# A fused attention layer on one core: the modulation and the first superblock's input by halves of the features, with the first halves of three chunks multiplied in between

## The chip, the cores and the metric

The kernel runs on one core of one Trainium2 chip. The metric is the device time of one execution in microseconds (us). Engines are named as the profile names them: PE is TensorE's matmul, PEld its weight load, DVE is VectorE, ACT is ScalarE, POOL is GpSimd, SP the engine that issues most DMAs.

## The reference

One decoder layer on x of 4096 rows and 1024 features:

```
shift, scale, gate = split(silu(c) @ w_ada + b_ada)
h    = rmsnorm(x, norm_g) * (1 + scale) + shift
proj = h @ w_in                      # 1024 x 3328, 26 chunks of 128 columns
y_sb = stick_breaking_attention(...) * silu(sb_g)     # 8 heads of 64
y_sw = sliding_window_sink_attention(...) * silu(sw_g) # 8 heads, 2 kv heads
x    = x + gate * (concat(y_sb, y_sw) @ w_out)
out  = rmsnorm(x, final_g)
```

The modulation needs c @ w_ada before the first h can be formed, and h before the first product with w_in.

## The kernel before

The rows are worked on in 8 superblocks of 512. Each matrix is split into two 16-bit parts, hi and lo, and a product is three passes: hi x hi, hi x lo, lo x hi. A chunk is 128 columns of w_in times the 512 rows: 8 feature tiles (k) x 3 passes = 24 matmuls of 128x128 by 128x512 into one PSUM bank (`mm`, four of them), written in items of two k. hT holds the superblock's input, transposed and split; w holds a chunk's weights, split by ACT (hi) and DVE (lo) in `stage_split`.

`setup_x0` makes the first superblock's hT. For the scale, then for the shift, DVE adds up eight rows blocks of w_ada, each times its element of silu(c), into `acc0` (`mod_part`, lines 125 and 127); `mod_cols` sums over the partitions on PE with a vector of ones (line 139, bank `pv`). With the scale, PE transposes the normalised rows and ACT writes xT (lines 171, 172); with the shift, ACT writes the hi part of hT (line 183) and DVE the lo part (line 184). a16 and s16, the scale and shift in columns, are also stored to DRAM (`arow`, `srow`, line 187), for the later superblocks.

For the first superblock the weights come from w_in in float32 (`stage_load`, line 273) through a ring `f` of four places, in the order `sorder`: SWK, SWG, SWG+1, SWG+2, SBV, SWQ, SBV+1, SWQ+1, SBV+2, SWG+3, SBV+3, SWV and so on. The four rows blocks of x take the same four places at first. The split weights lie in a ring `w` of three places, or for the v columns (SBV and its three followers, SWV) in `wv`; those of the ring are also stored to DRAM (`wsc`, line 293), for the later superblocks. `advance_w` loads one chunk and splits the oldest one loaded.

After `setup_x0`, `main` makes a list of work items: the chunks SWK, SWG, SWG+1, SWG+2, SWQ, then blocks of v (`v_items`, 24 matmuls each with all of SBV to SBV+3), further chunks, attention steps and output. On every second or fourth item a step of `setup_wo_items` is put in: eight loads of the gate's part of w_ada (`mod_load`, line 130), eight accumulates of the gate (lines 231 and 233) each followed by a load of w_out, a few small ones, and eight products of w_out with the gate (`wo`: two `wot` on DVE, line 254, then ACT and POOL). Near its end the first superblock's list also prepares the second superblock's input on PE (`x_items_pe`: `norm`, line 330, and transposes, line 400). Attention steps are placed among the items by times summed up from the items' estimates. Each engine runs its instructions in the order in which they are written; SP's DMAs share one queue.

Of the kernel before, what the change touches and what calls it, by code (L numbers as in the profile page):

```python
# [7 lines left out]
F32 = mybir.dt.float32  # L8
# [44 lines left out]
class Kern:  # L53
# [64 lines left out]

    def mod_part(self, which, k, st):

        nc = self.nc
        acc = self.acc0
# [11 lines left out]

    def mod_cols(self, which):
        nc = self.nc
        ps = self.P["pv"].tile([128, 512], F32, tag="pv", name="modps")
        for j in range(KD):
            nc.tensor.matmul(out=ps[:, j:j + 1], lhsT=self.acc0[:, j * 128:(j + 1) * 128], rhs=self.ones[:, 0:1],
                             start=True, stop=True)  # L140
        mod = self.const.tile([128, KD], F32, name=f"mod{which}")
        o = 16 + which * KD
        nc.vector.tensor_tensor(out=mod, in0=ps[:, 0:KD], in1=self.col[:, o:o + KD], op=ALU.add)
        return mod

    def setup_x0(self):

        nc = self.nc
        stage = self.wo.rearrange("p m e n -> p m (e n)").bitcast(F32)
        xs = [self.x_load(self.x[b * 128:(b + 1) * 128, :]) for b in range(2)]  # L150
        for k in range(KD):
            self.mod_load(1, k, stage[:, k])
        xs += [self.x_load(self.x[b * 128:(b + 1) * 128, :]) for b in range(2, NB)]
        xT = self.P["hT"].tile([128, KD, T], F32, tag="hT", name="xT")
        hT = self.new_hT(0)
        for b in range(2):
            self.x_norm(xs[b], hT[:, b, 0])
        self.run_later(9)
        for k in range(KD):
            self.mod_part(1, k, stage[:, k])  # L160
            self.mod_load(0, k, stage[:, k])
        for b in range(2, NB):
            self.x_norm(xs[b], hT[:, b, 0])
        self.run_later(9)
        scale = self.mod_cols(1)
        nc.vector.tensor_scalar(out=self.a16, in0=scale, scalar1=1.0, scalar2=HS, op0=ALU.add, op1=ALU.mult)
        nc.vector.tensor_tensor(out=self.a16, in0=self.a16, in1=self.col[:, 8:16], op=ALU.mult)
        for k in range(KD):
            ps = self.mm()
            for b in range(NB):  # L170
                nc.tensor.transpose(ps[:, b * 128:(b + 1) * 128], xs[b][:, k * 128:(k + 1) * 128], self.ident)
            nc.scalar.activation(xT[:, k, :], ps, AF.Identity, scale=self.a16[:, k:k + 1])
        self.stage_load()
        self.stage_load()
        self.stage_load()
        for k in range(KD):
            self.mod_part(0, k, stage[:, k])
        shift = self.mod_cols(0)
        self.stage_split()
        nc.vector.tensor_scalar(out=self.s16, in0=shift, scalar1=HS, scalar2=None, op0=ALU.mult)  # L180
        for k in range(KD):
            xk = xT[:, k, :].rearrange("p (b t) -> p b t", t=128)
            nc.scalar.activation(hT[:, :, 0, k, :], xk, AF.Identity, bias=self.s16[:, k:k + 1])
            nc.vector.scalar_tensor_tensor(out=hT[:, :, 1, k, :], in0=xk, scalar=self.s16[:, k:k + 1],
                                           in1=hT[:, :, 0, k, :], op0=ALU.add, op1=ALU.subtract)
        for row, col in ((self.arow, self.a16), (self.srow, self.s16)):
            nc.sync.dma_start(out=row.rearrange("o (k p) -> p (o k)", p=128), in_=col)
# [227 lines left out]

    def chunk_items(self, s, c, evac):
        nc = self.nc
# [298 lines left out]
    def main(self):  # L716
# [8 lines left out]
        self.sorder = [SWK, SWG, SWG + 1, SWG + 2, SBV, SWQ, SBV + 1, SWQ + 1, SBV + 2, SWG + 3, SBV + 3, SWV] + order[7:]  # L725
        self.spos, self.staged = [0, 0], []
        self.wpos = 0
# [8 lines left out]
        self.v[-1] = v0  # L736
        self.setup_x0()
        self.stage_load()
        self.stage_split()

# [19 lines left out]
        for s in range(NS):  # L760
# [15 lines left out]
            add([(0.0, lambda s=s: self.new_hT(s + 1))])  # L776
            step(self.chunk_items(s, SWK, self.evac_k(s, 4, "ksw")))
            for p in range(3):
                step(self.chunk_items(s, SWG + p, self.evac_g(s, 4 + p)))
            vi = self.v_items(s, s * NB)  # L780
# [279 lines left out]
```

## Time and profile before

| | |
|---|---|
| median of 3 runs | 1770.54 us (1769.33 to 1771.67) |
| the profiled execution | 1770.9 us, span 1769.2 us |
| PE busy | 1666.3 us (94%) |
| DVE, ACT, POOL busy | 1020.9, 725.0, 592.5 us |
| mean granted clock of PE | 0.98 |

Busy time is the time in which an engine works on an instruction; the span is that of the profiled execution on the chip, and about 1.7 us of its time lie around the span. A busy share over the whole span is a mean over stages with different limits.

### The profile page before, as it was taken

How to read it: one execution, taken by the hardware profiler on the slowest of the kernel's cores; microseconds unless marked ns; L12 is line 12 of the kernel's file. 1: busy time of each engine (PE TensorE's matmuls, PEld its weight loads, DVE VectorE, ACT ScalarE, POOL GpSimd, SP SyncE). 2: the span in 40 equal slices, each digit the busy share in tenths (PEclk: the TensorE clock that was granted, in tenths of full speed). 3: DMA queues.
4: the chain of work that ended last, by engine and by line, in shares of the span. 5: the costliest groups of instructions: out<-in, count | busy, mean ns of one | idle time of the engine just before them, and what ended most of it. 6: DMA issues, size and time to landing. Idle time of an engine off the chain costs nothing.

```text
span 1769.2 us, 28179 instructions
## 1 busy us (share of the span) xinstructions
PE 1666.3 (94%) x10790; PEld 859.7 (49%) x10790; DVE 1020.9 (58%) x1869; ACT 725.0 (41%) x1428; POOL 592.5 (33%) x745
## 2 busy tenths in 40 slices
PE   3798689999999999999999999999999999999987
PEld 2354345554554554554554445544545545545443
DVE  6467885565645566455645656455664557355562
ACT  3445653444335444343334443354433444244331
POOL 2023664432234323432234322442234323122231
PEclk9899879999999999999999999999999999999999
DMA  7877656466756757566665767567575756355552
GB/s 274 277 214 178 181 145 175 116 167 154 189 134 143 168 147 200 111 150 154 164 175 129 161 161 184 126 144 175 145 202 112 155 153 164 92 126 132 157 135 74
DMA packets 417126, 280.41 MB, mean 159 GB/s; under 512 B 341676, under 2 KB 368340, under 8 KB 416980
## 3 DMA queue, kind: packets, MB, share of 16 engines
q1 hardware_dynamic: 374692, 182.01, 44.0%
q10 hardware_dynamic: 42288, 96.49, 18.5%
q8 instruction: 87, 1.43, 0.3%
q14 instruction: 59, 0.48, 0.1%
HBM read 151.54 MB, written 27.80 MB: 101 GB/s over the span
## 4 chain that ended last, share of the span: by engine, by line
PE 74%; DVE 9%; ACT 6%; DMA 4%; POOL 3%; issue 3%; SPq 1%; ACTq 0%; POOLq 0%; DVEq 0%
PE mm L430 40%; PE mm L687 14%; PE mm L503 7%; PE pv L640 5%; PE z L555 4%; PE mm L515 2%; ACT p L599 2%; DMA q<-q 2%; DVE w L290 1%; DVE acc L127 1%; DMA f<-in_x_dram 1%; POOL p L608 1%; ACT hT L325 1%; DMA f<-in_w_in_dram 1%; DVE w L622 1%
## 5 line engine op out<-in xcount | busy, mean ns | idle before, releaser
L430 PE MATMUL mm<-hT,w 128*128 128x512 f16 x4032 | 914.2, 382 | 7.6 <-ACT w L289 2.8
L430 PEld LDWEIGHTS <-w 128*128 128x128 f16 x4032 | 389.0, 99 | 461.3 <-issue 17.6
L687 PE MATMUL mm<-wo,yT 128*128 128x512 f16 x1536 | 346.8, 381 | 0.0
L608 POOL TENSOR_SCALAR p<-p,smm 128x256 f32<-128x256 f32 x256 | 123.2, 502 | 432.8 <-DVE smm L606 302.9
L687 PEld LDWEIGHTS <-yT 128*128 128x128 f16 x1536 | 148.7, 98 | 171.7 <-issue 2.6
L658 POOL TENSOR_TENSOR yT<-gs,yT 128x256 f16<-128x256 f32 x128 | 142.7, 1115 | 248.4 <-DVE yT L657 233.6
L599 ACT ACTIVATE p<-sp,nm 128x256 f32<-128x256 f32 (+1 forms) x256 | 126.0, 493 | 222.2 <-DVE nm L592 222.0
L569 DVE TENSOR_TENSOR_SCAN nb<-nb,d 128x768 f32<-128x768 f32 x64 | 115.3, 1801 | 136.0 <-ACT nb L563 136.0
L565 POOL TENSOR_SCALAR_AFFINE_SELECT beta<-beta 128x512 f32<-128x512 f32 x64 | 90.2, 1410 | 283.4 <-ACT beta L564 243.1
L503 PE MATMUL mm<-wv,hT 128*128 128x512 f16 x768 | 174.9, 383 | 6.9 <-ACT wv L289 6.3
L503 PEld LDWEIGHTS <-hT 128*128 128x128 f16 x768 | 74.8, 98 | 93.6 <-issue 10.5
L622 DVE SCALAR_TENSOR_TENSOR w<-p,w 128x1024 f16<-128x1024 f32 x64 | 85.1, 1330 | 58.7 <-ACT w L621 58.7
L563 ACT ACTIVATE nb<-z 128x768 f32<-128x768 f32 x64 | 51.8, 810 | 160.4 <-PE z L555 93.0
L621 ACT ACTIVATE w<-beta 128x768 f16<-128x768 f32 x64 | 53.9, 842 | 153.8 <-DMA wT<-w 71.3
L640 PEld LDWEIGHTS <-v 128*64 128x64 f16 x2304 | 89.1, 110 | 55.3 <-issue 51.4
L592 DVE CUSTOM_DVE_ANT_0 sp<-z,bias,nsink 128x256 f32<-128x256 f32 (+1 forms) x256 | 107.2, 474 | 14.6 <-PE z L555 14.3
L640 PE MATMUL pv<-wT,v 128*64 128x128 f16 (+1 forms) x2304 | 110.1, 240 | 3.5 <-DVE yT L657 2.6
L621 ACT ACTIVATE w<-p 128x1024 f16<-128x1024 f32 x64 | 67.6, 1056 | 76.8 <-POOL p L608 39.7
L693 DVE SCALAR_TENSOR_TENSOR f<-mm,f 128x512 f32<-128x512 f32 x64 | 43.0, 675 | 86.9 <-DMA f<-in_x_dram 70.5
L494 DVE SCALAR_TENSOR_TENSOR v<-mm,v 128x512 f16<-128x512 f32 (+1 forms) x64 | 31.2, 488 | 97.3 <-ACT v L493 95.8
L555 PEld LDWEIGHTS <-q 128*128 128x128 f16 x768 | 68.4, 100 | 20.0 <-issue 3.2
L446 DVE SCALAR_TENSOR_TENSOR q<-mm,q 64x512 f16<-64x512 f32 x64 | 43.8, 684 | 59.2 <-ACT q L445 58.6
(113 smaller groups left out, 1737.1 us busy)
## 6 DMA issues: line engine op xcount, KB each, us to landing
w<-wsc ACTq DMA_DIRECT2D x147, 512.0 KB, 3.8
f<-in_x_dram SPq DMA_DIRECT2D x64, 512.0 KB, 4.6
q<-q ACTq DMA_DIRECT2D x128, 128.0 KB, 3.7
out_dram<-f SPq DMA_DIRECT2D x32, 512.0 KB, 3.6
f<-in_w_in_dram SPq DMA_DIRECT2D x26, 512.0 KB, 5.9
wo<-in_w_ada_dram SPq DMA_DIRECT2D x24, 512.0 KB, 8.0
wsc<-w SPq DMA_DIRECT2D x21, 512.0 KB, 5.3
wo<-in_w_out_dram SPq DMA_DIRECT2D x8, 512.0 KB, 5.7
```

Source lines behind the costliest of these rows:

```text
L430: nc.tensor.matmul(out=ps, lhsT=w[:, k, a, :], rhs=hT[:, :, b, k, :], start=(k == 0 and i == 0), stop=(k == KD - 1 and i == 2))
L503: nc.tensor.matmul(out=ps, lhsT=hT[:, tb, b, k, :], rhs=self.wv[:, k, a, 0:512], start=(k == 0 and i == 0), stop=(k == KD - 1 and i == 2))
L555: nc.tensor.matmul(out=o[:, k0:256], lhsT=q[:, j, h, cols], rhs=kt[:, kh, (qb - 1) * 128 + k0:(qb + 1) * 128], start=(j == 0), stop=(j == 1))
L569: nc.vector.tensor_tensor_scan(out=nbf, data0=nbf, data1=d1, initial=1.0, op0=ALU.mult, op1=ALU.max)
L592: nc.vector.tensor_tensor_reduce(out=sp[:, u, c0:256], in0=z[:, u, c0:256], in1=bias[:, c0:256], scale=-2.0 ** -(h + 1), scalar=self.nsink ...
L599: nc.scalar.activation(p[:, u, c0:256], sp[:, u, c0:256], AF.Exp, scale=-1.0, bias=nm[:, u:u + 1], accum_out=sm[:, u:u + 1])
L608: nc.gpsimd.tensor_scalar(out=p[:, u, :], in0=p[:, u, :], scalar1=sm[:, u:u + 1], scalar2=1.0, op0=ALU.mult, op1=ALU.mult)
L621: nc.scalar.activation(hi, w, AF.Copy, scale=WS)
L622: nc.vector.scalar_tensor_tensor(out=lo, in0=w, scalar=WS, in1=hi, op0=ALU.mult, op1=ALU.subtract)
L640: nc.tensor.matmul(out=pv[h * 64:(h + 1) * 64, o0:o0 + c1 - c0], lhsT=v[:, a, vc:vc + 64], rhs=wT[:, e, h, c0:c1], start=(n == 0 and i == ...
L658: nc.gpsimd.tensor_tensor(out=y[:, 1, cols], in0=y32, in1=y[:, 0, cols], op=ALU.subtract)
L687: nc.tensor.matmul(out=ps, lhsT=y[:, a, tb * 128:(tb + 1) * 128], rhs=self.wo[:, m, b, n * 512:(n + 1) * 512], start=(m == OORD[0] and i = ...
```

## The change

`setup_x0` runs twice over what it did once: for features 0 to 511 (e = 0), then 512 to 1023 (e = 1). In each half: the scale's columns, four transposes with xT, the shift's columns, four k of hT. w_ada comes in loads of 512 columns in place of 1024. The first three chunks' weights no longer come through the ring f but in halves into places of the later yT tiles (`first_load`), and are split in halves (`first_split`), with their wsc stores directly behind. After the first half of hT, the items k = 0 to 3 of the chunks SWK, SWG and SWG+1 are issued, into three banks; their other halves stand in the list as before. The second half's transposes use the banks `pv`. The ring f is loaded from SWG+2 on: three loads behind the second half's shift, and then two `advance_w` after each of the three chunks, in place of one or two within them. arow and srow are stored behind the three loads.

```
+    def first_split(self, i, sts, e):
...
+        nc.scalar.activation(dst[:, :, 0, :], sts[e], AF.Copy, scale=WS)
+        nc.vector.scalar_tensor_tensor(out=dst[:, :, 1, :], in0=sts[e], scalar=WS, in1=dst[:, :, 0, :],
+                                       op0=ALU.mult, op1=ALU.subtract)
+        if e:
+            nc.sync.dma_start(out=self.wsc[c][:], in_=w)
...
+        for e in range(2):
...
+            for k in range(KD):
+                self.mod_part(k, stage[:, k, 0:512], acc[:, 0:512])
+                if e == 0:
+                    load(1, 1, k)
...
+            scale = self.mod_cols(1, e, acc[:, 0:512])
...
+            for k in range(4 * e, 4 * e + 4):
+                ps = self.mm() if e == 0 else self.P["pv"].tile([128, 512], F32, tag="pv", name="xps")
...
+            for k in range(KD):
+                self.mod_part(k, stage[:, k, 512:1024], acc[:, 512:1024])
+                if e == 0:
+                    load(0, 1, k)
+            if e == 0:
+                self.first_split(0, first[0], 0)
+            else:
+                for _ in range(3):
+                    self.stage_load()
+            shift = self.mod_cols(0, e, acc[:, 512:1024])
...
+            if e == 0:
+                for i in (1, 2):
+                    self.first_split(i, first[i], 0)
+                for i in range(3):
+                    for f in heads[i][0:2]:
+                        f[1]()
+                for i in range(3):
+                    self.first_split(i, first[i], 1)
...
-                self.advance_w(s)
-            elif k0 == 4 and s == 0 and self.spos[1] < 13:
+            if not first and (k0 == 0 or (k0 == 4 and s == 0 and self.spos[1] < 13)):
                 self.advance_w(s)
...
+                if first:
+                    self.advance_w(s)
+                    self.advance_w(s)
```

How the instructions stand on DVE at the start, from the scale's accumulates on (L127 is an accumulate, L143 the column sums' end, L184 hT's lo part, L290 a lo split), before:

```order
L127 SCALAR_TENSOR_TENSOR acc_162<-wo,cond,acc_162 128x1024 x7
L330 TENSOR_SCALAR f<-f,r 128x1024 x2
L143 TENSOR_TENSOR mod_270<-modps,col 128x8
L166 TENSOR_SCALAR a_89<-mod_270 128x8
L167 TENSOR_TENSOR a_89<-a_89,col 128x8
L125 TENSOR_SCALAR acc_162<-wo,cond 128x1024
L127 SCALAR_TENSOR_TENSOR acc_162<-wo,cond,acc_162 128x1024 x7
L143 TENSOR_TENSOR mod_345<-modps,col 128x8
L290 SCALAR_TENSOR_TENSOR w<-f,w 128x8x128
L180 TENSOR_SCALAR s_90<-mod_345 128x8
L184 SCALAR_TENSOR_TENSOR hT<-xT,s_90,hT 128x4x128 x8
L290 SCALAR_TENSOR_TENSOR w<-f,w 128x8x128 x3
```

And on DVE of the changed kernel, from the first half's shift to the second half's scale (its lines 124, 126, 165 and 229 answer to 125, 127, 290 and 184):

```order
L124 TENSOR_SCALAR acc_162<-wo,cond 128x512
L126 SCALAR_TENSOR_TENSOR acc_162<-wo,cond,acc_162 128x512 x7
L165 SCALAR_TENSOR_TENSOR w<-first,w 128x4x128
L143 TENSOR_TENSOR mod_338<-modps,col 128x4
L225 TENSOR_SCALAR s_90<-mod_338 128x4
L229 SCALAR_TENSOR_TENSOR hT<-xT,s_90,hT 128x4x128 x4
L165 SCALAR_TENSOR_TENSOR w<-first,w 128x4x128 x5
L124 TENSOR_SCALAR acc_162<-wo,cond 128x512
L126 SCALAR_TENSOR_TENSOR acc_162<-wo,cond,acc_162 128x512 x7
L143 TENSOR_TENSOR mod_416<-modps,col 128x4
L207 TENSOR_SCALAR a_89<-mod_416 128x4
L208 TENSOR_TENSOR a_89<-a_89,col 128x4
```

The first half of hT, four steps, now stands ahead of the second half's accumulates, and five of the six half splits stand between the two; behind these rows come the second half's shift and its four steps of hT.

On SP's queue behind the shift's loads of w_ada, before (L273 is a load of w_in, L187 the stores of a16 and s16, L130 a gate load, L293 a wsc store):

```order
L273 DMA f<-in_w_in_dram 128x8x128 x3
L187 DMA arow<-a_89 128x8x1
L187 DMA srow<-s_90 128x8x1
L273 DMA f<-in_w_in_dram 128x8x128 x3
L130 DMA wo<-in_w_ada_dram 128x1024
L293 DMA wsc_76<-w 128x2048
L293 DMA wsc_77<-w 128x2048
L293 DMA wsc_78<-w 128x2048
L273 DMA f<-in_w_in_dram 128x8x128
L130 DMA wo<-in_w_ada_dram 128x1024
L293 DMA wsc_79<-w 128x2048
```

And of the changed kernel, at the same place (its lines 326, 240, 129 and 346 answer to 273, 187, 130 and 293; line 168 is the store in `first_split`):

```order
L168 DMA wsc_76<-w 128x2048
L168 DMA wsc_77<-w 128x2048
L168 DMA wsc_78<-w 128x2048
L326 DMA f<-in_w_in_dram 128x8x128 x3
L240 DMA arow<-a_89 128x8x1
L240 DMA srow<-s_90 128x8x1
L326 DMA f<-in_w_in_dram 128x8x128 x2
L129 DMA wo<-in_w_ada_dram 128x1024
L326 DMA f<-in_w_in_dram 128x8x128 x2
L129 DMA wo<-in_w_ada_dram 128x1024
L346 DMA wsc_79<-w 128x2048
L326 DMA f<-in_w_in_dram 128x8x128 x3
```

The three stores have moved ahead of the ring's loads and of arow and srow; the three loads ahead of arow are now those of SWG+2, SBV and SWQ, where they were those of the first three chunks. Counted from srow, the load of SBV+3 (the first of the last three shown) was the 18th transfer on this queue and is now the 8th.

## Rows read from the trace of the kernel before

**Rows 1.** The page's busy times, and its granted clock of PE in 40 equal slices, in tenths.

```profile
PE 1666.3 (94%) x10790; PEld 859.7 (49%) x10790; DVE 1020.9 (58%) x1869; ACT 725.0 (41%) x1428; POOL 592.5 (33%) x745
PEclk9899879999999999999999999999999999999999
```

**Rows 2.** Busy time of each engine by stretches of 10 us (length, then us and instructions of each engine), with PE's granted clock, the DMA engines' mean busy share and GB/s at the end.

```profile
60.00:70.00 10.00, 6.50 (x24) 2.31 (x23) 5.64 (x7) 5.67 (x7) 0.00 (x0) 0.83 1.05 374
70.00:80.00 10.00, 7.07 (x33) 3.12 (x32) 4.20 (x5) 3.31 (x4) 0.00 (x0) 1.00 1.04 340
80.00:90.00 10.00, 5.99 (x17) 2.11 (x17) 5.42 (x7) 4.01 (x6) 0.00 (x0) 0.66 1.09 363
```

**Rows 3.** DVE's instructions in order of time at the start: start us, us, engine, line, operation, out<-in, form, count, and the idle time before with what ended it.

```profile
13.33 0.75 DVE L125 TENSOR_SCALAR acc<-wo,cond 128x1024 f32<-128x1024 f32 x1
14.11 9.21 DVE L127 SCALAR_TENSOR_TENSOR acc<-wo,cond,acc 128x1024 f32<-128x1024 f32 x7
...
23.24 0.75 DVE L330 TENSOR_SCALAR f<-f,r 128x1024 f32<-128x1024 f32 x1
...
26.98 0.17 DVE L143 TENSOR_TENSOR mod<-modps,col 128x8 f32<-128x8 f32 x1 [1.75 <-PE modps L139]
...
43.20 5.39 DVE L184 SCALAR_TENSOR_TENSOR hT<-xT,s,hT 128x512 f16<-128x512 f32 x8 [0.85 <-ACT hT L183]
48.51 2.35 DVE L290 SCALAR_TENSOR_TENSOR w<-f,w 128x1024 f16<-128x1024 f32 x2
```

**Rows 4.** PE's matmuls in order of time to 98 us, same columns.

```profile
23.38 3.57 PE L139 MATMUL modps<-ones,acc 128*128 128x1 f32 x16 [19.90 <-DVE acc L127]
26.81 5.68 PE L171 MATMUL mm<-ident,f 128*128 128x128 f32 x32
...
43.22 0.59 PE L430 MATMUL mm<-hT,w 128*128 128x512 f16 x1 [2.30 <-ACT hT L183]
44.00 17.43 PE L430 MATMUL mm<-hT,w 128*128 128x512 f16 x71 [0.20 <-DVE hT L184]
...
64.28 0.60 PE L430 MATMUL mm<-hT,w 128*128 128x512 f16 x2 [2.84 <-ACT w L289]
65.54 11.53 PE L430 MATMUL mm<-hT,w 128*128 128x512 f16 x46 [0.66 <-DVE w L290]
83.33 0.58 PE L503 MATMUL mm<-wv,hT 128*128 128x512 f16 x1 [6.27 <-ACT wv L289]
84.59 11.14 PE L503 MATMUL mm<-wv,hT 128*128 128x512 f16 x41 [0.68 <-DVE wv L290]
...
97.64 0.22 PE L548 MATMUL z<-kp,q 128*128 128x128 f16 x1 [1.86 <-DMA q<-q]
```

**Rows 5.** The two accumulates of the gate at 512 columns, from DVE's instructions in order of time, same columns.

```profile
88.74 0.87 DVE L231 TENSOR_SCALAR gb<-wo,cond 128x512 f32<-128x512 f32 x2
...
91.08 1.41 DVE L233 SCALAR_TENSOR_TENSOR gb<-wo,cond,gb 128x512 f32<-128x512 f32 x2
```

**Rows 6.** SP's issues in order of time; then the DMA issues of 30 to 46 us by line (count, KB each, us from issue to landing); then stretches, columns as in rows 2.

```profile
32.19 2.11 SPq L273 DMA_DIRECT2D f<-in_w_in_dram  x3
34.40 1.50 SPq L187 DMA_DIRECT2D arow<-a  x1
42.38 0.37 SPq L187 DMA_DIRECT2D srow<-s  x1
42.84 11.02 SPq L273 DMA_DIRECT2D f<-in_w_in_dram  x3
...
arow<-a SPq DMA_DIRECT2D x1, 4.0 KB, 13.6
srow<-s SPq DMA_DIRECT2D x1, 4.0 KB, 11.3
...
44.00:48.00 4.00, 4.00 (x10) 1.43 (x10) 4.00 (x7) 4.00 (x7) 0.00 (x0) 0.50 0.02 0
48.00:53.00 5.00, 5.00 (x25) 2.25 (x23) 2.86 (x3) 1.35 (x2) 0.00 (x0) 1.00 0.23 32
...
56.00:82.00 26.00, 17.57 (x74) 7.22 (x72) 11.46 (x12) 9.81 (x12) 0.00 (x0) 0.93 1.06 352
```

**Rows 7.** Two splits on ACT in order of time (of the fourth chunk and of SBV+3), and the copies of q in the chain of work that ended last (start us, us, what).

```profile
63.17 1.06 ACT L289 ACTIVATE w<-f 128x1024 f16<-128x1024 f32 x1 [13.82 <-DMA wsc<-w]
...
82.23 1.06 ACT L289 ACTIVATE wv<-f 128x1024 f16<-128x1024 f32 x1 [1.40 <-DMA f<-in_w_in_dram]
...
91.08 6.43 DMA q<-q
```

**Rows 8.** Two stretches of 1 us, columns as in rows 2; the granted clock is the third number from the end.

```profile
38.00:39.00 1.00, 1.00 (x6) 1.00 (x6) 0.00 (x0) 0.00 (x0) 0.00 (x0) 0.50 1.22 252
48.00:49.00 1.00, 1.00 (x7) 0.42 (x5) 1.00 (x2) 1.00 (x2) 0.00 (x0) 1.00 0.31 46
```

**Rows 9.** Where PE waits for the second superblock's normalisation, and two pairs of `wot` on DVE, in order of time.

```profile
223.22 0.47 PE L400 MATMUL mm<-ident,f 128*128 128x128 f32 x1 [8.64 <-DVE f L330]
252.09 0.45 PE L400 MATMUL mm<-ident,f 128*128 128x128 f32 x1 [5.22 <-DVE f L330]
...
221.22 1.28 DVE L254 TENSOR_TENSOR wot<-wo,gb 128x512 f32<-128x512 f32 x2
228.97 2.25 DVE L254 TENSOR_TENSOR wot<-wo,gb 128x512 f32<-128x512 f32 x2
```

More of the change, by code (lines that the diff above doesn't have):

```diff
@@ L117, in setup_small, with mod_part @@
         self.col, self.cond = col, cond
-    def mod_part(self, which, k, st):
+    def mod_part(self, k, st, acc):
         nc = self.nc
-        acc = self.acc0
         ck = self.cond[:, k:k + 1]
@@ L133, in bc, with mod_cols @@
         return self.P["bc"].tile([128, D], F32, tag="bc", name=name)
-    def mod_cols(self, which):
+    def mod_cols(self, which, e, acc):
         nc = self.nc
         ps = self.P["pv"].tile([128, 512], F32, tag="pv", name="modps")
-        for j in range(KD):
-            nc.tensor.matmul(out=ps[:, j:j + 1], lhsT=self.acc0[:, j * 128:(j + 1) * 128], rhs=self.ones[:, 0:1],
+        for j in range(4):
+            nc.tensor.matmul(out=ps[:, j:j + 1], lhsT=acc[:, j * 128:(j + 1) * 128], rhs=self.ones[:, 0:1],
@@ L140, in mod_cols @@
                              start=True, stop=True)
-        mod = self.const.tile([128, KD], F32, name=f"mod{which}")
-        o = 16 + which * KD
-        nc.vector.tensor_tensor(out=mod, in0=ps[:, 0:KD], in1=self.col[:, o:o + KD], op=ALU.add)
-        return mod
-    def setup_x0(self):
+        mod = self.const.tile([128, 4], F32, name=f"mod{which}{e}")
+        o = 16 + which * KD + 4 * e
+        nc.vector.tensor_tensor(out=mod, in0=ps[:, 0:4], in1=self.col[:, o:o + 4], op=ALU.add)
+        return mod
@@ new lines, in first_load @@
+    def first_load(self, i):
+        c = self.sorder[i]
+        out = []
+        for e in range(2):
+            t = self.P["yT"].pool.tile([128, 4, 128], F32, tag=f"yT{2 * i + e}", name="first")
+            self.nc.sync.dma_start(out=t, in_=self.w_in[e * 512:(e + 1) * 512, c * 128:(c + 1) * 128].rearrange(
+                "(k p) n -> p k n", p=128))
+            out.append(t)
+        return out
+    def first_split(self, i, sts, e):
+        nc = self.nc
+        c = self.sorder[i]
+        if e == 0:
+            self.wq[(0, c)] = self.P["w"].tile([128, KD, 2, 128], F16, tag="w", name="w")
+        w = self.wq[(0, c)]
+        dst = w[:, 4 * e:4 * e + 4]
+        nc.scalar.activation(dst[:, :, 0, :], sts[e], AF.Copy, scale=WS)
[3 more added lines that the diff above has]
+            nc.sync.dma_start(out=self.wsc[c][:], in_=w)
@@ L148, in setup_x0, with load @@
+    def setup_x0(self, heads):
         nc = self.nc
         stage = self.wo.rearrange("p m e n -> p m (e n)").bitcast(F32)
+        acc = self.acc0
+        def load(which, e, k):
+            o = which * D + e * 512
+            nc.sync.dma_start(out=stage[:, k, (1 - which) * 512:(2 - which) * 512],
+                              in_=self.w_ada[k * 128:(k + 1) * 128, o:o + 512])
         xs = [self.x_load(self.x[b * 128:(b + 1) * 128, :]) for b in range(2)]
         for k in range(KD):
-            self.mod_load(1, k, stage[:, k])
+            load(1, 0, k)
@@ L153, in setup_x0 @@
         xs += [self.x_load(self.x[b * 128:(b + 1) * 128, :]) for b in range(2, NB)]
+        for k in range(KD):
+            load(0, 0, k)
+        first = [self.first_load(0), self.first_load(1)]
         xT = self.P["hT"].tile([128, KD, T], F32, tag="hT", name="xT")
         hT = self.new_hT(0)
[L156 to L172, printed above, removed]
@@ L413, in x_items_pe, with chunk_items @@
                 [(440.0, lambda g=g, k=k: tr(g, k)) for k in range(0, KD, 2)] for g in range(2)]
-    def chunk_items(self, s, c, evac):
+    def chunk_items(self, s, c, evac, first=False):
         nc = self.nc
@@ L736, in main @@
         self.v[-1] = v0
-        self.setup_x0()
-        self.stage_load()
-        self.stage_split()
+        heads = [self.chunk_items(0, c, ev, first=True) for c, ev in
+                 ((SWK, self.evac_k(0, 4, "ksw")), (SWG, self.evac_g(0, 4)), (SWG + 1, self.evac_g(0, 5)))]
+        self.setup_x0(heads)
         fill = []
@@ L776, in main @@
             add([(0.0, lambda s=s: self.new_hT(s + 1))])
-            step(self.chunk_items(s, SWK, self.evac_k(s, 4, "ksw")))
+            step(self.chunk_items(s, SWK, self.evac_k(s, 4, "ksw")) if s else heads[0][2:])
             for p in range(3):
-                step(self.chunk_items(s, SWG + p, self.evac_g(s, 4 + p)))
+                step(heads[p + 1][2:] if s == 0 and p < 2 else self.chunk_items(s, SWG + p, self.evac_g(s, 4 + p)))
             vi = self.v_items(s, s * NB)
```

40 lines of the change are left out of this document (26 added, 14 removed).

## The prediction

> **What bounds the kernel now.** I read the page first: TensorE (PE) is busy for 94% of the span, and its granted clock falls below full only in the first slices [rows 1]. So the question is where PE stands idle, and the table of ten-microsecond stretches says that much of it is at the start: between 60 and 90 us it is busy 6 to 7 of every 10 us, while the DMA engines are at full share [rows 2]. The timeline of PE then gives the path. Nothing is multiplied until 43.2 us; three chunks run to 61.43 (44.00 + 17.43); PE waits 2.84 and 0.66 us for the fourth chunk's weights, 6.27 and 0.68 us before the first v block, and 1.86 us for a copy of q [rows 4]. The timeline of VectorE (DVE) shows that the first 43 us belong to it: eight accumulates for the scale, eight for the shift, two waits for column sums, then the eight hT steps that end at 48.59 (43.20 + 5.39) [rows 3]. What ends the later waits is the DMA side: the fourth chunk's split waited 13.82 us for a wsc store, and the split of SBV+3, which the v block needs, for its load at 82.23 [rows 7]. These loads are late for a reason that the stretches show: after the stores of arow and srow, 4 KB each in 4-byte pieces, which take 13.6 and 11.3 us to land, the engines move 0 GB/s from 44 to 48 us and 32 GB/s to 53, although loads stand in the queue; from 56 to 82 they run full at 352 GB/s [rows 6].
>
> **The change on DVE and PE.** A pass of eight accumulates of half width costs 0.87 / 2 + 7 x 1.41 / 2 = 5.4 us, by the same two forms at 512 columns [rows 5], against 0.75 + 9.21 = 9.96 at full width [rows 3]; four half passes make 21.5 us in place of 19.9. From 13.33 us, which nothing in the change moves: scale half to 18.7; two normalisations (0.75 each and a wait) to 20.3; four column sums, 3.57 / 2 = 1.8 us, to 20.5; the small steps, 0.5, to 21.0; shift half to 26.4; column sums and s16 to 28.5, under which one half split lies; ScalarE's lead of 0.85 and four hT steps of 5.39 / 8 = 0.67 to 32.1; five half splits of 2.35 / 4 = 0.6 to 35.2; then the second halves: scale to 40.6, sums and small steps to 42.9, shift to 48.3, sums and s16 to 50.4, and hT from 51.3 to 54.0. All prices are from [rows 3, 4]. So hT is complete 5.4 us later than before. The loads of these halves are no bound: they are issued as the accumulates free their places, from 13 to 26 us, and used from 35 on; the halves of ACT's splits and transposes lie under DVE's passes.
>
> PE multiplies the first halves, 36 matmuls, from 29.4 us: even at 0.427 us each for the first twelve and 0.217 after (of the 17.43 us of 71 matmuls, [rows 4], about ten lie in the slow 4 us from 44 to 48, [rows 6], and 61 in the 13.4 after; the slow pace is about twice the fast one) it is done by 40, before the next column sums need it at 40.6. So this work is hidden, and moves nothing by itself. The second halves are another 36, from 51.3. Before, the clock was at half by 38 us, after PE had stood, and full again at 48, five microseconds into the matmuls [rows 8]. Taking the same, twelve slow (5.1 us) and 24 fast (5.2) end at 61.6, against 61.43. **The three chunks end when they did.** The bounds: all fast, 59.1 (hT then gates them); all slow, 66.7.
>
> **What lies behind the three chunks** is where time can be won. Their wsc stores are now issued by 36 us, into idle DMA, and no longer stand before the fourth chunk's weights. The first three ring loads wait for the second transposes, which end at about 45.9 (from 42.5, four groups of 5.68 / 8 = 0.71, held up by ACT through two buffers), and land by 52. ACT evicts ksw after chunk 0 (56.4), and the fourth chunk's weights are ready at about 60: no wait, so that chunk and SWQ run to 61.6 + 48 x 0.217 = 72.0, where they ended at 77.07 (65.54 + 11.53).
>
> The next loads are another matter. arow and srow now stand behind the three ring loads and before all others on SP's queue. Before, the first ring load went out at 32.19, arow landed at 48.0 and srow 5.7 us after it [rows 6]. With the first ring load at 45.9, arow lands at 61.7, and srow at 67.4 if it drains after arow, or at 62.0 if its own 11.3 us from 50.7 hold. I take 65; the loads behind, issued from 51 on, run then. Up to SBV+3's load the queue holds five w_in loads, two gate loads and one store: 8 x 0.524 MB = 4.2 MB, 11.9 us at 352 GB/s, so it lands at 77 (74 to 79.5), against 82.23. Before, SP's order has 18 transfers from srow to that load (eight w_in loads, five gate loads, five stores), now eight: three loads and three stores are done ahead of the hole, the other gate loads come six work items later. Its ACT split (1.06) and DVE split (1.2) bring the v blocks to full pace at 79.3, against 84.59: **5.3 us**. The copies of q follow two loads later (3.0 us), a split, the eviction (about 2.6) and 6.43 us of flight [rows 7], at about 90.1; the v blocks, 11.14 us as before, also end at 90.4, so the 1.86 us wait goes too: up to 7.2 us at z, where it stood at 97.64. I take 6.
>
> **What is moved later.** The list of gate and w_out steps keeps its beats, but six items of matmuls left the list, so each step comes about 7.8 us of work later. Until 140 us this falls on a DVE with room. In the stretch that prepares the second superblock, two wot pairs change sides of the first normalisation, for which PE waits 8.64 us at 223: before it they free 2 x 1.28 = 2.6 us, behind it one pair (up to 2.25) lies ahead of the second x load, for which PE waits 5.22 us at 252 [rows 9]. I count this as 0, between -2.6 and +2.6. POOL gets no work and no wait. Extra instructions (24 on DVE, 19 DMA issues) are inside the sums above; SP has its 46 issues done by the time DVE frees the places.
>
> **Sum.** 1770.9 (the profiled execution, 0.4 above the median 1770.54) + 0 (hT is 5.4 us later, but the chunks end as before) - 6 (v blocks and q) + 0 (steps moved later) = 1764.9, given as **1765.0 us**.
>
> **Rivals.** (a) The scattered stores do not hold the queue in the new place. Then the load after next goes out at 60.3, when the fourth chunk's split frees its place, and SBV+3 is the seventh from there: 60.3 + 7 x 0.524 / 0.352 = 70.7, with a little flight 72. The v blocks run from 74.3 and z from 86: 10 to 12 us, 1759 to 1761. Against it: two landings of over 11 us with an idle DMA side. (b) No change: the hole ends later. At 70 us SBV+3 lands at 82 and all is won back. That needs the drains in series and a head 3 us longer; 0.1 us more on each of 28 half accumulates makes 2.8. Or the wot steps take 2.6 and the hole ends at 67: 1768 to 1771. (c) Slower: the clock stays at half from 51.3 on, since PE is in pieces with waits between. 84 matmuls at 0.427 end at 87.2 instead of 77.07, the v blocks begin there, 2.6 us after 84.59, and at half clock cost 42 x 0.427 - 11.14 = 6.8 more: 1774 to 1780. It decides only beyond 63 slow matmuls of the 84 (51.3 + 63 x 0.427 + 21 x 0.217 = 82.8, and the split of SBV+3 was the bound until then). Against it: before, full clock came back after five microseconds of matmuls, and the second pass runs without a wait for 20 us.
>
> On (c) the Trainium skill speaks: "TensorE: Matmul & The Clock Gate", section "HAM oscillation — how this bites in real kernels", says that bursts of matmuls parted by long waits each start at the low clock. The rows at 38 and 48 us agree. By that rule both passes start slow, as I have taken them, and the sum stays; only if PE never ran long enough would (c) follow.
>
> **How the numbers follow.** Chances: forecast, with the hole's end between 62 and 67, 0.55 (1761 to 1768); (a) 0.15; (b) 0.20; (c) 0.10. The range 1757 to 1771.5 takes in the forecast, (a), (b) and the 2.6 us of the moved steps on the fast side, and leaves out (c) and the corners of the others. 0.2% of the time is 3.5 us, about what can be told from no change: below 1767.0 lie (a) and most of the forecast, 0.63; within it the rest of the forecast and (b), 0.27; above it 0.10.
>
> **What would show it.** Right: 36 matmuls from about 29.4 us; hT complete near 54; the third chunk's end within 2 us of 61.6; no wait before the fourth; arow and srow landing between 60 and 68 with little moved in the microseconds before; the first v matmuls at 78 to 80; z near 90. Wrong: the v blocks before 76 (the hole is not real) or after 83; half clock beyond 57 us; waits at the second superblock's transposes that grow by more than 2.6 us.

## Result and the profile after

The changed kernel takes **1789.79 us** (median of 5 runs, 1788.8 to 1791.46), against 1770.54 (5 runs beside them, 1769.33 to 1775.23): a ratio of 1.0105, 95% interval 1.0092 to 1.0117. It is 19 us slower, where the prediction had 1765.0 us and a range up to 1771.5. The profiled execution has a span of 1789.0 us against 1769.2.

The page of after, busy times and granted clock, against [rows 1]; under it the stretches of [rows 2] in the changed kernel:

```profile
PE 1669.1 (93%) x10790; PEld 858.7 (48%) x10790; DVE 1020.5 (57%) x1893; ACT 723.4 (40%) x1431; POOL 579.0 (32%) x745
...
PEclk9899989999999999999999999999999999999999
```

```profile
60.00:70.00 10.00, 10.00 (x48) 4.51 (x47) 8.00 (x9) 6.19 (x8) 0.00 (x0) 1.00 0.85 214
70.00:80.00 10.00, 5.12 (x23) 2.14 (x22) 4.30 (x5) 4.21 (x5) 0.00 (x0) 1.00 1.12 318
80.00:90.00 10.00, 9.95 (x39) 4.20 (x39) 4.64 (x6) 3.52 (x6) 0.00 (x0) 0.83 1.04 372
```

The start became what it was meant to be. PE is busy for 25 of the 30 us from 60 to 90, where it was busy for 19.6. Its timeline, against [rows 4]:

```profile
31.45 9.74 PE L482 MATMUL mm<-hT,w 128*128 128x512 f16 x35 [0.20 <-DVE hT L229]
...
53.96 20.78 PE L482 MATMUL mm<-hT,w 128*128 128x512 f16 x83 [0.20 <-DVE hT L229]
78.79 0.38 PE L558 MATMUL mm<-wv,hT 128*128 128x512 f16 x1 [4.04 <-ACT wv L342]
80.05 10.64 PE L558 MATMUL mm<-wv,hT 128*128 128x512 f16 x41 [0.88 <-DVE wv L343]
...
95.45 0.27 PE L603 MATMUL z<-kp,q 128*128 128x128 f16 x1 [4.71 <-DMA q<-q]
```

The 36 first-half matmuls end at 41.2 us, the wait before the fourth chunk is gone, and the v blocks are at full pace at 80.05, 4.5 us earlier than before. The first z is only 2.2 us earlier, after a wait of 4.71 us for a copy of q. From there on everything is lost and more.

To see where, I use a mark that both kernels have in the same order: ScalarE (ACT) evicting the scores of a block for a scan (`nb<-z`), the first, eighth, ninth and 57th of 64. They start at 183.93, 283.27, 420.20 and 1650.63 us before the change, and **11.84, 18.59, 20.34 and 21.84 us later** after it. The eighth, before and after, with the wait ahead of it:

```profile
283.27 0.81 ACT L563 ACTIVATE nb<-z 128x768 f32<-128x768 f32 x1 [3.95 <-PE z L555]
...
301.86 0.81 ACT L618 ACTIVATE nb<-z 128x768 f32<-128x768 f32 x1 [4.29 <-PE mm L482]
```

So 18.6 of the loss stand by 283 us, in the first superblock's attention and the making of the second superblock's input, where PE multiplies the same things in the same order in both kernels; the 1370 us from there to the last mark add 3.3, and 2.0 come back behind it (the span is 19.8 us longer).

The waits there are spread over many lines, which names no culprit. First PE's waits of before, then of after, from 60 to 330 us (sum, times, longest; nm is written by the softmax step on DVE, line 592 before and 647 after):

```profile
PE mm L400 <- DVE f L330: 15.4, 4, 8.6
PE mm L503 <- ACT wv L289: 6.3, 1, 6.3
PE z L548 <- DMA q<-q: 6.1, 4, 3.0
PE z L548 <- DVE nm L592: 3.6, 1, 3.6
```

```profile
PE mm L453 <- DVE f L383: 19.7, 4, 9.7
PE z L603 <- DMA q<-q: 10.0, 5, 4.7
PE z L603 <- DVE nm L647: 7.9, 2, 5.3
PE mm L482 <- DVE hT L462: 3.7, 1, 3.7
PE z L610 <- DVE nm L647: 3.1, 1, 3.1
```

The groups of ACT in the same window name it, again before, then after:

```profile
L289 ACT ACTIVATE w<-f 128x1024 f16<-128x1024 f32 x18 | 18.9, 1049 | 25.7 <-DMA wsc<-w 13.8 <-DMA f<-in_w_in_dram 6.3 <-DVE q L448 3.0
...
L563 ACT ACTIVATE nb<-z 128x768 f32<-128x768 f32 x8 | 6.4, 805 | 8.2 <-PE z L555 8.1
```

```profile
L342 ACT ACTIVATE w<-f 128x1024 f16<-128x1024 f32 x18 | 19.0, 1053 | 24.7 <-PE mm L482 9.3 <-DMA wsc<-w 7.5 <-DVE q L503 6.1
...
L618 ACT ACTIVATE nb<-z 128x768 f32<-128x768 f32 x8 | 6.4, 802 | 15.9 <-PE mm L482 15.8
```

The same 18 splits and 8 evictions; but the splits of `w` now wait 9.3 us for **matmuls of chunks** (`mm L482`), which end none of their waits before, and the evictions of z wait 15.8 us not for z but for chunk matmuls, with which they have nothing to do. Something that stands ahead of them in ACT's queue does. The experiments say what.

### The profile page after: what moved, and what is told of

The parts are those of the page before. It is cut to its first block, busy times and chain, and to the rows that moved or that the text cites. A ratio compares the mean times of both kernels' runs of the same rounds, so it can differ in the third digit from the quotient of the medians.

```text
span 1789.0 us, 28323 instructions
## 1 busy us (share of the span) xinstructions
PE 1669.1 (93%) x10790; PEld 858.7 (48%) x10790; DVE 1020.5 (57%) x1893; ACT 723.4 (40%) x1431; POOL 579.0 (32%) x745
## 4 chain that ended last, share of the span: by engine, by line
PE 69%; DVE 8%; DMA 8%; ACT 7%; POOL 3%; issue 2%; SPq 1%; ACTq 0%; POOLq 0%; DVEq 0%
PE mm L482 38%; PE mm L742 14%; PE mm L558 5%; PE pv L695 4%; DMA q<-q 4%; PE z L610 4%; PE mm L570 2%; ACT p L654 2%; ACT hT L378 1%; DMA f<-in_x_dram 1%; POOL p L663 1%; DMA wo<-in_w_ada_dram 1%; DVE w L343 1%; DVE nb L624 1%; DVE w L677 1%
## 5 line engine op out<-in xcount | busy, mean ns | idle before, releaser
L482 PE MATMUL mm<-hT,w 128*128 128x512 f16 x4032 | 915.4, 382 | 10.5 <-DVE hT L462 3.7
L482 PEld LDWEIGHTS <-w 128*128 128x128 f16 x4032 | 389.6, 99 | 464.6 <-issue 26.6
L713 POOL TENSOR_TENSOR yT<-gs,yT 128x256 f16<-128x256 f32 x128 | 134.3, 1049 | 246.8 <-DVE yT L712 246.7
L647 DVE CUSTOM_DVE_ANT_0 sp<-z,bias,nsink 128x256 f32<-128x256 f32 (+1 forms) x256 | 107.1, 474 | 9.4 <-PE z L610 9.0
L677 DVE SCALAR_TENSOR_TENSOR w<-beta,w 128x768 f16<-128x768 f32 x64 | 61.1, 954 | 35.7 <-ACT w L676 35.7
```

The costliest lines, as they stand in the source:

```text
L482: nc.tensor.matmul(out=ps, lhsT=w[:, k, a, :], rhs=hT[:, :, b, k, :], start=(k == 0 and i == 0), stop=(k == KD - 1 and i == 2))
L647: nc.vector.tensor_tensor_reduce(out=sp[:, u, c0:256], in0=z[:, u, c0:256], in1=bias[:, c0:256], scale=-2.0 ** -(h + 1), scalar=self.nsink ...
L677: nc.vector.scalar_tensor_tensor(out=lo, in0=w, scalar=WS, in1=hi, op0=ALU.mult, op1=ALU.subtract)
L713: nc.gpsimd.tensor_tensor(out=y[:, 1, cols], in0=y32, in1=y[:, 0, cols], op=ALU.subtract)
```

## The experiments

Ratios are to runs of the kernel before on the same chip, with 95% intervals; 0.2% can be told from no change. "Marks" are the four of above, against the one profile of before. The medians of before differ by 2.2 us between the groups of runs (1770.54 to 1772.77), so a difference of two or three us in a mark is no more than a hint. "Lead" is how far the splits of `w` run ahead of the chunk being multiplied, and the loads ahead of the splits.

### Which part: the steps six items late, or the lead of the splits

The two `advance_w` behind each of the first three chunks and the three loads ahead of them leave the splits of `w` one step of the list ahead of before, and the loads three ahead of the splits where before had two. I had noted the first only as the reason for "no wait". The other suspect was the term that the prediction had set to 0.

Steps of `setup_wo_items` back by six items (the lead stays):

```
-        beat = [0]
+        beat = [6]
+        for _ in range(2):
+            fill.append((0.0, extra.pop(0), -1))
```

> The changed kernel, with the 27 steps of setup_wo_items put back to the places that they have before the change relative to the multiplications (the counter of items starts at 6, and the first two gate loads stand ahead of the list). Loads and splits of w stay one ahead, as in the changed kernel. Theory S (the loss comes from these steps coming six items later, so that on DVE the bcast and the gate accumulates stand right ahead of the softmax step L647 and the wot products stand between the second superblock's transposes): nearly all of the 19.3 us come back, 1766 to 1774 us, and the waits of z on DVE nm at 153 and 165 us (3.07 and 5.29 us in the changed kernel) shrink to before's one of 3.6. Theory L (the loss comes from the loads and splits being one chunk further ahead, three f tiles held): 1785 to 1792 us. Theory R (the arow and srow stores hold the SP queue's later loads and transfers back): 1785 to 1792 us.

Measured: 1791.52 us, **1.0098** (1.0081 to 1.0115). Nothing came back.

The kernel before with its steps six items late (`beat = [-6]`, and no step while the counter is not positive):

> The kernel before the change, with only the 27 steps of setup_wo_items placed six items later (the counter of items starts at -6), all else as before. Theory S: slower by most of the loss, 1783 to 1794 us, with a wait of z on DVE nm near 160 us and longer waits of the second superblock's transposes on DVE. Theories L and R: as before, 1768 to 1774 us.

Measured: 1773.72 us, **1.0004** (0.9995 to 1.0014). As the cause of the 19 us, theory S falls by both. (The marks of the second are 5.38, 5.53, 6.39 and 4.30 us late in the profiled execution; the timed runs show no such loss.)

The lead of loads and splits back (the steps stay late):

```
-                for _ in range(3):
+                for _ in range(2):
                     self.stage_load()
...
                 if first:
                     self.advance_w(s)
-                    self.advance_w(s)
+                    if c != SWK:
+                        self.advance_w(s)
```

> The changed kernel, with loads and splits of w put back to the lead that they have before the change (two f loads ahead of the list where the change has three, and one split fewer after the first chunk), the 27 steps left six items late. Theory S: 1785 to 1792 us. Theory L: 1766 to 1774 us. Theory R: 1785 to 1792 us.

Measured: 1771.7 us, **0.9995** (0.9985 to 1.0005). The whole loss is gone: theory L.

Both back:

> The changed kernel with both put back, the 27 steps and the lead of loads and splits: from the fourth chunk on DVE and ScalarE then run the same list as before the change, and only the first 80 us differ. Theory S: 1764 to 1771 us, with or without the lead, so the gain of the head (4.5 us at the first v product, 2.2 us at the first z) is what is left. Theory L: the same time, but then the run with the lead alone put back gives it too. Theory R, or a loss that comes from the head itself: 1783 to 1792 us.

Measured: 1772.5 us, **0.9996** (0.9985 to 1.0007). As fast as the run before it, so the steps' place shows in neither time (what it gives and takes inside them stands further down). But it is above what any theory had for it, 1771 at most: the head's gain is gone as well. PE's timeline of this run says why:

```profile
72.47 0.60 PE L482 MATMUL mm<-hT,w 128*128 128x512 f16 x2 [2.69 <-ACT w L342]
...
85.25 0.58 PE L559 MATMUL mm<-wv,hT 128*128 128x512 f16 x1 [5.10 <-ACT wv L342]
```

Without any lead both waits of [rows 4] are back, 2.69 for the fourth chunk (2.84 before) and 5.10 for wv (6.27 before).

### Which half of the lead: splits or loads

> The changed kernel with the f loads back at before's lead over the splits (two ahead where the change has three), but the splits still one item of the list ahead of before. The run with both put back settled that the loss comes from this lead; two mechanisms are left. Theory W (the ring of w has 3 tiles: a split one chunk earlier writes the tile that the chunk being multiplied still reads, so ScalarE, which works in order, stands at the split, and later at the w prefetch, until TensorE has finished that chunk, and the evacuations of nb and beta behind it are late): still slow, 1783 to 1794 us. Theory F (the ring of f has 4 tiles: with three w loads ahead, the x loads of the second superblock find no free tile, SP stands about 10 us at 211.68 us, and what is queued behind it is late): 1766 to 1775 us.

The edit is the first of the two of the run with the lead back. Measured: 1795.58 us, **1.0129** (1.0101 to 1.0157): still slow, a little slower than theory W's numbers.

> The other half: the changed kernel with the splits back at before's places, but the f loads still three ahead of the splits. Theory W: 1766 to 1775 us. Theory F: 1783 to 1794 us, with SP standing some 10 us at the second superblock's first x loads.

The second edit alone. Measured: 1768.84 us, **0.9975** (0.9965 to 0.9985): fast. The two groups of ACT, of the run with the splits ahead and then of the one with the loads ahead:

```profile
L342 ACT ACTIVATE w<-f 128x1024 f16<-128x1024 f32 x18 | 19.0, 1054 | 28.7 <-DMA f<-in_w_in_dram 12.8 <-PE mm L482 9.7 <-DVE q L503 6.2
...
L618 ACT ACTIVATE nb<-z 128x768 f32<-128x768 f32 x8 | 6.4, 802 | 15.7 <-PE mm L482 15.7
```

```profile
L342 ACT ACTIVATE w<-f 128x1024 f16<-128x1024 f32 x18 | 18.9, 1051 | 11.8 <-DVE q L504 6.2 <-DMA f<-in_w_in_dram 5.5
...
L619 ACT ACTIVATE nb<-z 128x768 f32<-128x768 f32 x8 | 6.5, 806 | 8.1 <-PE z L611 8.1
```

The waits on chunk matmuls come and go with the splits' lead. Theory F's own sign goes the other way: SP's issues of the second superblock's first x loads stand 9.81 us in the fast run and 1.67 in the slow one:

```profile
197.01 9.81 SPq L371 DMA_DIRECT2D f<-in_x_dram  x2
```

```profile
214.92 1.67 SPq L371 DMA_DIRECT2D f<-in_x_dram  x2
```

So a full ring of x and w loads, which looks as bad, costs nothing here that can be told from no change.

### Why: three tiles of w

`w` is a ring of three (`BUFS`: `w=3`). Before, the first item of chunk n splits chunk n+2, into the tile of chunk n-1, whose matmuls are done. One step ahead it splits n+3, into the tile that chunk n itself is reading. The program text of the two kernels has it: of the 189 splits and prefetches of `w` on ACT 4 wait on a semaphore of PE (a counter that PE raises as it finishes matmuls) before the change, and 162 of 192 after it; 1 in the run with the lead back. (21 of each count belong to a branch that these executions don't enter, and none of those waits on PE: the trace has 147 prefetches, and after the change all 147 wait on PE.) Two of them, of before and of after (operation and what it waits for):

```
ACTIVATE w<-f 128x8x128 [waits DMAHW3_49]
DMA w<-wsc_76 128x2048 [waits DMAHW7_49]

ACTIVATE w<-f 128x8x128 [waits DMAHW5_49,PE_49]
DMA w<-wsc_76 128x2048 [waits DMAHW6_49,PE_49]
```

What it does in the first superblock, in the changed kernel's timeline (all engines):

```profile
107.94 1.04 PE L610 MATMUL z<-ksw,q 128*128 128x256 f16 x8
108.81 2.75 PE L482 MATMUL mm<-hT,w 128*128 128x512 f16 x12
...
111.60 1.06 ACT L342 ACTIVATE w<-f 128x1024 f16<-128x1024 f32 x1 [3.87 <-PE mm L482]
112.69 1.23 DVE L343 SCALAR_TENSOR_TENSOR w<-f,w 128x1024 f16<-128x1024 f32 x1 [4.63 <-ACT w L342]
113.83 1.41 DVE L286 SCALAR_TENSOR_TENSOR gb<-wo,cond,gb 128x512 f32<-128x512 f32 x2
115.16 0.48 DVE L647 CUSTOM_DVE_ANT_0 sp<-z,bias,nsink 128x256 f32<-128x256 f32 x1
```

z is done at 108.98. ACT stands at the split until the chunk's last matmul, at 111.56; DVE stands at its half of the split for ACT; and the softmax step L647, which needs only z, starts at 115.16, 6.2 us after z. The same place in the run where both leads are taken back at SWQ (1767.32 us, below):

```profile
101.90 1.04 PE L610 MATMUL z<-ksw,q 128*128 128x256 f16 x8
102.57 1.05 ACT L342 ACTIVATE w<-f 128x1024 f16<-128x1024 f32 x1
...
103.65 1.23 DVE L343 SCALAR_TENSOR_TENSOR w<-f,w 128x1024 f16<-128x1024 f32 x1 [0.65 <-ACT w L342]
...
106.11 0.48 DVE L647 CUSTOM_DVE_ANT_0 sp<-z,bias,nsink 128x256 f32<-128x256 f32 x1
```

There the split waits for nothing and the softmax starts 3.2 us after z. PE's waits in the changed kernel then carry other names, q copies and nm, so the list of its waits doesn't name the cause.

Once the splits are done the prefetches of `w` for the second superblock inherit the place. They are issued from ACT's queue, and the issue waits in the same way:

```profile
270.26 1.24 PE L610 MATMUL z<-ksb,q 128*128 128x192 f16 x8
271.34 4.05 PE L482 MATMUL mm<-hT,w 128*128 128x512 f16 x18
...
275.42 0.33 ACTq L350 DMA_DIRECT2D w<-wsc  x1
275.79 0.81 ACT L618 ACTIVATE nb<-z 128x768 f32<-128x768 f32 x1 [4.10 <-PE mm L482]
276.64 1.76 DVE L624 TENSOR_TENSOR_SCAN nb<-nb,d 128x768 f32<-128x768 f32 x1 [3.95 <-ACT nb L618]
...
281.98 2.79 DVE L462 CAST hT<-h 128x256 f16<-128x256 f32 x4
...
283.45 0.38 PE L482 MATMUL mm<-hT,w 128*128 128x512 f16 x1 [3.67 <-DVE hT L462]
```

z ends at 271.50, the chunk at 275.39, the prefetch goes out at 275.42, and only then are the scores evicted; the scan, hT behind it on DVE, and PE's wait of 3.67 us follow.

How the loss divides between splits and prefetches:

```
+        elif s == 0 and self.wpos == 0 and not self.skipped:
+            self.skipped = True
         elif s != "G" and self.wpos < len(self.worder):
             self.w_prefetch(*self.worder[self.wpos])
```

> The changed kernel with the first prefetch of a w tile left to the next call: all the splits of the first superblock are one ahead as in the changed kernel, all prefetches after them stand where before has them. Theory W by the marks of the scans: of the 19.3 us some 8 lie in the splits, 6.5 in the first prefetches (250 to 275 us) and 5 in the later ones, so this run should come to 1775 to 1782 us. If the splits carry all of it: 1787 to 1792 us; if the prefetches do: 1765 to 1771 us.

Measured: 1779.66 us, **1.0048** (1.0031 to 1.0065); marks 12.73, 12.48, 13.40 and 9.59. So the splits carry about 8.5 us of the loss, the prefetches the other 10 or so, by the difference of the two runs.

The lead alone, in the kernel before (one further load and split ahead of the list):

```
-        self.stage_load()
-        self.stage_split()
+        for _ in range(2):
+            self.stage_load()
+            self.stage_split()
```

> The kernel before the change with one further load and split of w ahead of the list, and nothing else: the lead of the changed kernel without its halves. Theory W: slower, 1783 to 1797 us, since from the second w tile on each split and prefetch waits for TensorE, as in the changed kernel. If the lead costs only together with the halves' head: 1768 to 1775 us.

Measured: 1797.81 us, **1.0143** (1.0125 to 1.0162), a little above theory W's numbers; 165 of its 189 splits and prefetches wait on PE. The halves are not needed for the loss. The run with the splits ahead alone, which has the same lead and the halves, has 1.0129 with an interval that overlaps this one, so it can't be told whether the halves hide any of it. A fourth tile in `w`, which would test the ring by itself, was not run.

### What the change is worth without it

The lead kept until wv is split, then taken back (`self.spos[1] < 12` in place of 13 in `part`):

> The changed kernel with one extra split fewer at the chunk SWQ (the bound 13 on the position is 12): the splits keep the change's lead until the last slice of wv is split, ahead of the v products, and stand where before has them from there on. Loads stay three ahead. Theory W: 1763 to 1771 us, because the head keeps its 4.5 us at the first v product and no later split or prefetch waits for TensorE. Theory F: 1783 to 1794 us.

Measured: 1769.33 us, **0.9981** (0.9972 to 0.9991).

The loads' lead taken back too (no `stage_load` at position 12):

> As the run before it, and one load is left out at the same place, so that the loads too fall back to before's lead of two. Theories W and F both: 1762 to 1771 us; if W alone is true it equals the run before it within 0.2 per cent.

Measured: 1767.32 us, **0.9964** (0.9953 to 0.9975). Both are faster than before. Between the two the intervals overlap: the second median is 2.0 us less on the same chip, 0.11%.

The stores of arow and srow in rows of 512 bytes, in this last kernel and in the kernel before:

```
+            ps = self.P["pv"].tile([128, 512], F32, tag="pv", name="rowps")
+            nc.tensor.transpose(ps[0:KD, 0:128], col, self.ident)
+            r = self.acc0[0:KD, i * 128:(i + 1) * 128]
+            nc.vector.tensor_copy(r, ps[0:KD, 0:128])
-            nc.sync.dma_start(out=row.rearrange("o (k p) -> p (o k)", p=128), in_=col)
+            nc.sync.dma_start(out=row.rearrange("o (k p) -> (o k) p", p=128), in_=r)
```

> The run with the lead taken back after the v products (1767.32 us), and arow and srow stored as eight rows of 512 bytes (each column pair is transposed on TensorE first and copied by DVE) instead of as 1024 pieces of 4 bytes. Theory R' (the small stores keep the transfers queued behind them on SP from starting for some 10 us, and the loads of the fourth chunk and of wv come late by that): the f loads behind the stores land some 10 us sooner, and the first v product, which waits for no split then, moves by what it waits for now; 1762 to 1766 us. If these loads are early enough as it is (three of them are ahead): 1766 to 1769 us.

Measured: 1765.26 us, **0.9961** (0.9947 to 0.9975): no more than without. (The number lies in the range of theory R', but before has 1771.58 us on this chip, where it had 1772.76 beside the run without.) Its v blocks did move, from a wait of 5.70 us to 2.88, but that is not kept.

> The kernel before the change with only the stores of arow and srow changed in that way. There the wait of the v products for the split of wv at 83.33 us is 6.27 us, and the split waits for a load behind the stores. Theory R': that wait shrinks by several us and z comes earlier by as much, 1764 to 1770 us. If the loads are late for another reason (all queues together move too many bytes): 1769 to 1774 us.

Measured: 1767.69 us, **0.9977** (0.9966 to 0.9989), faster, though not as said: the wait for wv did not shrink but grew to 7.64 us, and it ends at 80.21 instead of 83.33, since the fourth chunk came earlier (its waits for weights went from 2.84 and 0.66 us to 0.66 in all).

### Where the head's gain goes

In the run with the loads ahead alone (0.9975) z comes 8.4 us early (its rows stand in the next section), yet its marks are only 2.96, 0.23, 0.66 and 1.84 us early. In it, with and without row stores, and in the run with both leads taken back at SWQ the late steps were put back to the places that before has.

> The run with the splits on before's places and the f loads three ahead (0.9975; its first z stood 8.4 us earlier than before the change, at 89.27 us, but its scans at 283 us only 0.2), now also with the 27 steps of setup_wo_items put back by six items. Theory S' (the steps' later place takes the head's gain away before 190 us, as the kernel before with its steps six items late shows it: 5.4 us late at the first scan, 184 us): the first scan moves from 181.0 to about 176 us and the time comes to 1761 to 1766 us. Theory G (the gain is lost at the second superblock's x loads and transposes, where TensorE waits for the normalised x whenever it comes): scans at 283 us stay within 1.5 us, time 1766 to 1771 us.

Measured: 1770.72 us, **0.9989** (0.9980 to 0.9998), slower than without (0.9975). Marks 2.41 early, then 2.85, 3.51 and 1.76 late. Neither theory, though the time lies in G's range: the gate loads now stand ahead of wv's loads on SP again, and the v blocks wait 8.00 us:

```profile
81.72 0.58 PE L559 MATMUL mm<-wv,hT 128*128 128x512 f16 x1 [8.00 <-ACT wv L342]
```

> The run before it, with arow and srow stored in rows of 512 bytes. If the stores still hold the loads of wv back: 1 to 3 us less than the run before it. If the three loads ahead have taken that wait away: the same time within 0.1 per cent.

Measured: 1764.88 us, **0.9955** (0.9941 to 0.9969), 5.8 us less than the run before it where 1 to 3 was said; marks 7.74, 2.82, 3.23 and 6.16 early. With the stores out of the way the v blocks start at 77.47 in spite of the gate loads, and most of the gain is still there at the last mark. This is the fastest median of all runs, though the 1765.26 us above can't be told from it.

> The run in which loads and splits fall back to before's lead at SWQ (0.9964), with the 27 steps put back by six items. Theory S': 3 to 5 us less, 1761 to 1765 us by its own kernel before. Theory G: 1766 to 1770 us.

Measured: 1767.57 us, **0.9968** (0.9958 to 0.9978), as without. The steps' place gives at one end what it takes at the other: the v blocks start at 83.30 us after a wait of 9.04 us, where they start at 79.43 after 5.70 without; and from 60 to 330 us PE waits 15.7 us for the normalised x and 3.6 for nm, where it waits 19.8 and 8.0.

That holds for every run. With the steps six items late (nine kernels) PE waits 18.7 to 20.7 us for the second superblock's normalised x in that stretch, and 7.7 to 11.2 for nm; with the steps in their old place (eight kernels) 14.3 to 16.9 and 3.6 to 4.8. The kernel before with nothing but late steps shows it alone: 15.4 becomes 19.9, 3.6 becomes 8.4. So in the run with the loads ahead, where the two are 20.7 and 9.2 (14.3 and 3.8 with the steps back), the late steps cost more waiting than the 8.4 us that z was early. What stays open is the rest: in the fastest run the steps are in place (15.8 and 3.9), and 7.74 us early at the first mark still become 2.82 at the eighth.

## Why the prediction was wrong

**The step that failed** is "ACT evicts ksw after chunk 0 (56.4), and the fourth chunk's weights are ready at about 60: no wait", in the part on what lies behind the three chunks. What was read there is true, there is no wait. But it was booked as a gain only. The splits that are done early are done one chunk ahead for good, and the sum has no term for what a split one chunk ahead waits for in a ring of three. "What is moved later ... I count this as 0" looked at the other half of the same shift, the one with DVE's work. The missing term is +19 to +26 us (the changed kernel against the run with the lead back, and the lead alone in the kernel before), three to over four times the 6 us that the sum was made for. Where the loads stand alike, the splits' lead is worth 23 or 24 us (1.0129 against 0.9995, and 1.0105 against 0.9975). No rival had it: above the range stood only the half clock, (c), which was wrong too, as PE ran at full clock from 60 to 80 us in the rows above.

The other steps, one by one:

- **DVE.** A half pass was put at 5.4 us and took 6.0 (0.48 + 5.48 and the gap between them), four times. The price of 512 columns was read from two gate accumulates that stood in one row of the timeline [rows 5], 0.71 each; seven in a row cost 0.78 each. hT was complete at 55.9, not 54.0:

```profile
44.45 5.48 DVE L126 SCALAR_TENSOR_TENSOR acc<-wo,cond,acc 128x512 f32<-128x512 f32 x7
...
53.16 2.74 DVE L229 SCALAR_TENSOR_TENSOR hT<-xT,s,hT 128x512 f16<-128x512 f32 x4 [0.85 <-ACT hT L228]
```

- **PE's first halves** were hidden, from 30.66 to 41.19 (29.4 to 40), and the second halves, the fourth chunk and SWQ ran in one piece to 74.74, 2.7 us later than the 72.0 said. hT's 1.9 are a part; the other 0.8 is about what the clock makes, granted at half (0.50) until 59.4 us, some 17 matmuls where twelve were taken. So "half clock beyond 57 us", one of the signs of being wrong, came true, but it is not where the 19 us went.
- **The hole.** SP issued arow at 47.87 and srow at 52.34; the engines then moved little until about 63 (the 132 GB/s of the 6 us from 60 are what 352 GB/s, the full rate of [rows 6], move in 2.3), for the 65 taken:

```profile
53.00:60.00 7.00, 6.62 (x17) 2.27 (x17) 2.74 (x4) 3.10 (x6) 0.00 (x0) 0.54 0.32 16
60.00:66.00 6.00, 6.00 (x30) 2.70 (x29) 5.56 (x6) 4.60 (x7) 0.00 (x0) 1.00 0.69 132
```

- **v and z.** Full pace at 80.05 for 79.3 said. z came at 95.45 for about 90: the split one step ahead stood in front of q's eviction on ACT, and waited 4.00 us for the store of the tile that it was to fill:

```profile
84.50 1.06 ACT L342 ACTIVATE w<-f 128x1024 f16<-128x1024 f32 x1 [4.00 <-DMA wsc<-w]
87.56 1.48 ACTq L518 DMA_DIRECT2D q<-q  x2
```

  Without that split, in the run with the loads ahead alone, the v blocks are at full pace at 78.95 and z at 89.27, so the 5.3 and "up to 7.2" (measured 5.6 and 8.4) were well sized:

```profile
78.95 9.01 PE L559 MATMUL mm<-wv,hT 128*128 128x512 f16 x41 [0.89 <-DVE wv L343]
89.27 0.22 PE L604 MATMUL z<-kp,q 128*128 128x128 f16 x1 [1.25 <-DMA q<-q]
```

- **From z to the end** the sum took the head's gain as lasting. Without the lead of the splits the time falls by 0.25% (4.4 us) there, and by 0.36% (6.4 us) where both leads are taken back at SWQ, of the 6 booked.
- **Steps six items late**: 0 is what the time shows (1.0004), but not because they meet room. PE's waits for the normalised x grew from 15.4 to 19.7 us, more than the 2.6 allowed, which was another sign of being wrong; the kernel before with late steps has 19.9, and is 5.38 us late at the first mark of its profiled execution. In place, the gate loads stand ahead of the wv loads instead (the wait of 8.00 us).

The Trainium skill's sentence on bursts parted by waits ("TensorE: Matmul & The Clock Gate", section "HAM oscillation — how this bites in real kernels") held as it was used: both passes began at the low clock (granted clock 0.50 from 30 to 34 us and again from 53 to 57, by stretches of 4 us) and full clock came back.

## What to carry to other kernels

When work is taken out of a list that also drives a prefetch, ask what distance the prefetch now keeps, and hold it against the number of tiles in the ring it writes: at a distance equal to the ring, each prefetch waits for the work that is running, and everything behind it in its engine's queue waits too. It shows before any run: look in the changed program at what the prefetching instructions wait for, and count those that got a new partner (here from 4 to 162). In a trace it shows as an engine waiting for results that its own instruction doesn't read.

## What the runs showed of the hardware

- A DMA issue that waits for its tile holds up the compute behind it on the same engine: behind three prefetches of the changed kernel ACT's evictions of z waited 4.10, 7.44 and 4.29 us for chunk matmuls that they don't read.
- The same waits cost far less in the later superblocks: from the ninth mark to the last the changed kernel, all of whose prefetches wait on PE, loses 1.5 us in 1230, and the run whose prefetches stand where before has them gains 3.8. No run shows why so little.
- Two 4 KB stores in 512-byte rows in place of 4-byte pieces were worth 0.23% (0.11 to 0.34) of the kernel before; in 4-byte pieces they took 13.6 and 11.3 us to land [rows 6].
- SP standing 9.81 us at two loads left nothing in the time that can be told (0.9975, against 0.9995 in the run with the lead back).
